# WKV recurrence in chunks: 126 steps with a head against 128 steps with carries in a spare row

## The chip, the cores and the metric

The kernel runs on one core of a Trainium2 chip. The metric is the device time in microseconds (us), the median over runs; a profile of one execution gives the span of the program's instructions on top of it.

## What is computed

The reference is a recurrence over time, for each of 16 batches and 256 columns, with a running maximum that keeps the exponentials in range:

```python
batch, seq_len, d_model = (16, 2048, 256)
for b in range(batch):
    aa = 0; bb = 0; pp = -1e38              # state: numerator, denominator, exponent
    for t in range(seq_len):
        kk = k[b, t]; vv = v[b, t]
        ww = u + kk
        qq = maximum(pp, ww)
        e1 = exp(pp - qq); e2 = exp(ww - qq)
        output[b, t] = (e1 * aa + e2 * vv) / (e1 * bb + e2 + 1e-08)
        ww = pp - w + kk                    # the reference's own recurrence
        qq = maximum(ww, kk)
        e1 = exp(ww - qq); e2 = exp(kk - qq)
        aa = e1 * aa + e2 * vv
        bb = e1 * bb + e2
        pp = qq
```

Note that kk is added to the exponent of the old state too, so the exponent of a state entry is a running sum of k and w. Inputs and output are fp32, 33.6 MB each for k, v and the output.

## The kernel before

Time lies on the partitions, batch and column on the free axis. A chunk is TC = 126 time steps, two halves of HS = 63; 2048 = 16 x 126 + 32, and the first 32 steps are a "head", worked three batches' groups at a time on 96 partitions. A pair is four batches of one chunk, a tile of 126 rows by 1024 columns (128 rows are loaded, two of them replaced). So there are two pairs for the head and four for each of the 16 chunks: 66 pairs, and the main loop has one slot for each, then ten more for the outputs, which run LAG = 9 slots behind.

In one slot n of the loop, in the order of the source, which is also the order on each engine's own queue:

- load(n + 3): two transfers of 512 KB, k and v, issued by GpSimd (L106).
- exps(n), ScalarE (L238): exp of 2048 columns of X, from PSUM, to bf16. X holds two sets of exponents, one as seen from later steps (E) and one with u for the step itself (Z).
- gather_factors (L295, L301), every second slot: rows 126 and 127 of ez, which hold the factors over a half, go by SyncE's transfers to 64 partitions by 64 columns.
- sums(n - 1), TensorE (L279): four one-hot matmuls add the sums of ez and ez*v over each half into one PSUM tile, a row for each.
- round_k(n + 1), VectorE (L219): k to the rounded fp32 form that TensorE takes.
- num(qp, 0), den(q), recip(q), mult(qp, 0), num(qp, 1), mult(qp, 1): the outputs of older pairs, qp = n - 10 and q = n - 9. den and num are matmuls with a triangular matrix and the identity (L399, L417), recip is Ln and Exp on ScalarE (L407, L408), mult the product on VectorE (L428). num has a single PSUM buffer.
- times_v(n), VectorE (L254): ez * v for both sets.
- store, every second slot: 1008 KB, by GpSimd (L444).
- logs(n + 1), TensorE (L227): the exponents as a matmul of k, w and u with constant matrices; X has one buffer of four PSUM banks.
- cast_v(n + 1), VectorE (L246): v to bf16.

Between these stand the steps of the state, spread over the slots after a chunk's last pair by the table `later`: copy_sums (VectorE, L306, and four transfers L311 from rows to 64 partitions), state_logs, state_weights and inject_logs on ScalarE, state_offsets and inject_min on VectorE (L331 to L335, L370, L372), state_chain and inject on GpSimd (L355 to L360, L383), and at the end eight transfers (L387) that write the carries into rows 126 and 127 of the chunk's own ez tiles, from where den and num take them up. [...]

```python
work = [(s + 1, "sums", copy_sums), (s + 2, "exp", state_logs), (s + 2, "dve", state_offsets),
        (s + 2, "act", state_weights), (s + 3, "pool", state_chain)]
if c >= 0:
    work += [(s + 3, "act", inject_logs), (s + 4, "first", inject_min),
             (s + 4, "exp", inject_weights), (s + 4, "pool", inject)]
```

Of the kernel before, what the change touches and what calls it, by code (L numbers as in the profile page):

```python
# [7 lines left out]
F32 = mybir.dt.float32  # L8
# [4 lines left out]

# [3 lines left out]
def kernel(  # L23
# [13 lines left out]
    HS = 63  # L37
    TC = 2 * HS
    T0 = T % TC
    NST = T // TC  # L40
    D = 2 * Dm
    GB = T0
    NG = 3
    NH = NG * GB
    AHEAD = 3
    LAG = 9
    RS = 2.0 ** -43
    LNRS = 43 * 0.6931471805599453
    CAP = 68.0

    consts = ctx.enter_context(tc.tile_pool(name="consts", bufs=1))
    kpool = ctx.enter_context(tc.tile_pool(name="kpool", bufs=AHEAD + 1))
    vpool = ctx.enter_context(tc.tile_pool(name="vpool", bufs=AHEAD + 1))
    vbpool = ctx.enter_context(tc.tile_pool(name="vbpool", bufs=2))
    ezpool = ctx.enter_context(tc.tile_pool(name="ezpool", bufs=6))
    rpool = ctx.enter_context(tc.tile_pool(name="rpool", bufs=3))
# [6 lines left out]
    pst = ctx.enter_context(tc.tile_pool(name="pst", bufs=1, space=bass.MemoryType.PSUM))  # L63
# [4 lines left out]
    pairs = [("head", 0), ("head", 1)]  # L68
    for c in range(NST):
        for p in range(4):  # L70
            pairs.append((c, p))
    NP = len(pairs)
    kr_of, vr_of = {}, {}

    def is_head(n):
        return n < 2

    def tiles_of(n):
        return 1 if n == 1 else 2

    def head_view(x, g):
        b = 6 * g
        e = min(b + 6, B)
        return e - b, x[b:e, 0:T0, :].rearrange("n t d -> t n d")

    def load(n):
        kr = kpool.tile([128, 4, Dm], F32, tag="kr", name="kr")
        vr = vpool.tile([128, 4, Dm], F32, tag="vr", name="vr")
        kr_of[n], vr_of[n] = kr, vr
        if is_head(n):  # L90
            if n == 1:
                K(DVE.memset(kr[64:96, 0:2, :], 0.0))
                K(DVE.memset(vr[64:96, 0:2, :], 0.0))
            for t, x, eng in ((kr, k, SP), (vr, v, SC)):
                for g in range(NG):
                    b = 6 * g + 4 * n
                    e = min(b + 2 * tiles_of(n), B)
                    if b < e:
                        K(eng.dma_start(out=t[g * GB:(g + 1) * GB, 0:e - b, :],
                                        in_=x[b:e, 0:T0, :].rearrange("n t d -> t n d")))  # L100
        else:
            c, p = pairs[n]
            t0 = T0 + c * TC
            r = min(128, T - t0)
            for t, x in ((kr, k), (vr, v)):
                K(POOL.dma_start(out=t[0:r, :, :],  # L106
                               in_=x[4 * p:4 * p + 4, t0:t0 + r, :].rearrange("n t d -> t n d")))

    crow = opool.tile([128, 8, Dm], F32, tag="ot", name="crow")[:, 0:4, :]
    K(DVE.memset(crow[96:128], 0.0))  # L110
    load(0)
    for r, x in ((NH, w), (NH + 1, u), (TC, w), (TC + 1, u)):
        K(POOL.dma_start(out=crow[r:r + 1, :, :], in_=bass.AP(
            tensor=x.tensor, offset=x.offset, ap=[[0, 1], [0, 4], list(x.ap[0])])))
    for n in range(1, AHEAD):
        load(n)


    M1 = consts.tile([128, 128], F32, tag="M1", name="M1")
    I1 = consts.tile([128, 128], F32, tag="I1", name="I1")  # L120
    cc = consts.tile([128, 8], F32, tag="cc", name="cc")
    GE, NE = ALU.is_ge, ALU.not_equal

    def select(ap, cmp, fill, base, cm, n, step):
        K(POOL.affine_select(out=ap, in_=ap, pattern=[[step, n]], compare_op=cmp,
                             fill=fill, base=base, channel_multiplier=cm))

    IO = consts.tile([128, 128], F32, tag="IO", name="IO")
    IOh = consts.tile([128, 128], F32, tag="IOh", name="IOh")
    K(POOL.memset(M1, -1.0))  # L130
    select(M1, GE, 0.0, -1, -1, 128, 1)
    K(POOL.memset(I1, 0.0))
    select(I1, NE, 1.0, 0, -1, 128, 1)
    K(POOL.memset(cc, 0.0))
    for j, r in enumerate((NH, NH + 1, TC, TC + 1)):
        select(cc[:, j:j + 1], NE, 1.0, r, -1, 1, 0)
    K(POOL.memset(cc[:, 4:5], 0.5))
    select(cc[:, 4:5], GE, 0.0, -HS, 1, 1, 0)
    select(cc[:, 4:5], GE, 0.0, TC - 1, -1, 1, 0)
    K(POOL.iota(IOh[:, 0:NH], pattern=[[0, NG], [1, GB]], base=0, channel_multiplier=0,  # L140
                allow_small_or_imprecise_dtypes=True))
    K(POOL.iota(IO[:, 0:TC], pattern=[[0, 2], [1, HS]], base=0, channel_multiplier=0,
                allow_small_or_imprecise_dtypes=True))
# [7 lines left out]
    def head_blocks(f):  # L151
        fill(f[0:GB, GB:NH], 0.0)
        fill(f[GB:2 * GB, 2 * GB:NH], 0.0)

    def step_matrices(name, rows, N, io):
        E, Z = matrix("NLE" + name, F32R), matrix("NLZ" + name, F32R)
        cw, cu = cc[:, rows:rows + 1], cc[:, rows + 1:rows + 2]
        K(DVE.scalar_tensor_tensor(E[:, 0:N], io[:, 0:N], cw, M1[:, 0:N], ALU.mult, ALU.add))  # L160
        K(DVE.scalar_tensor_tensor(Z[:, 0:N], I1[:, 0:N], cu, E[:, 0:N], ALU.add, ALU.add))
        K(DVE.tensor_scalar(E[:, 0:N], E[:, 0:N], cw, None, ALU.add))
        return E, Z

    NLEh, NLZh = step_matrices("h", 0, NH, IOh)
    for f in (NLEh, NLZh):
        head_blocks(f)
        fill(f[:, NH:128], 0.0)
    for g in range(NG):
        fill(NLEh[g * GB:(g + 1) * GB, NH + g:NH + g + 1], 0.5)  # L170
    K(DVE.tensor_single_scalar(NLEh[96:98, NH:NH + NG], cc[96:98, 0:1].broadcast_to([2, NG]),
                               -0.5 * GB, op=ALU.mult))
    kms = [consts.tile([128, 4, Dm], F32R, tag=f"km{j}", name=f"km{j}") for j in range(2)]
    for t in kms:
        K(DVE.tensor_copy(t[96:128, :, :], crow[96:128, :, :]))

    def more_matrices():
        NLE, NLZ = step_matrices("", 2, TC, IO)
        for f in (NLE, NLZ):
            fill(f[0:HS, HS:TC], 0.0)  # L180
            fill(f[:, TC:128], 0.0)
        K(DVE.tensor_single_scalar(NLE[96:128, TC:128], cc[96:128, 2:3].broadcast_to([32, 2]),
                                   -0.5 * HS, op=ALU.mult))
        fill(NLE[0:HS, TC:TC + 1], 0.5)
        K(DVE.scalar_tensor_tensor(NLE[:, TC + 1:128], cc[:, 2:3], -0.5 * HS, cc[:, 4:5], ALU.mult, ALU.add))
        OHh = consts.tile([128, 256], BF16, tag="OHh", name="OHh")
        fill(OHh, 0.0)
        for g in range(NG):
            fill(OHh[g * GB:(g + 1) * GB, 128 + 3 * g:129 + 3 * g], 1.0)
        OH = consts.tile([128, 256], BF16, tag="OH", name="OH")  # L190
        fill(OH, 0.0)
        fill(OH[0:HS, 128:129], 1.0)
        fill(OH[:, 136:137], 1.0)
        fill(OH[0:HS, 136:137], 0.0)
        Id, IdN, Lh, LhN, Lf, LfN = [matrix(x, BF16) for x in ("Id", "IdN", "Lh", "LhN", "Lf", "LfN")]
        K(DVE.tensor_copy(Id, I1))
        K(DVE.tensor_single_scalar(IdN, I1, RS, op=ALU.mult))
        for t, s in ((Lh, 1.0), (LhN, RS)):
            K(DVE.tensor_single_scalar(t, M1, -s, op=ALU.mult))
            head_blocks(t)  # L200
            fill(t[:, NH:128], 0.0)
        Lx = matrix("Lx", F32)
        K(DVE.tensor_scalar(Lx, M1, -1.0, None, ALU.mult))
        fill(Lx[0:HS, HS:TC], 0.0)
        K(DVE.tensor_scalar(Lx[:, 0:HS], Lx[:, 0:HS], cc[:, 2:3], None, ALU.add))
        K(DVE.tensor_scalar(Lx[:, HS:TC], Lx[:, HS:TC], cc[:, 3:4], None, ALU.add))
        fill(Lx[:, TC:128], 0.0)
        K(DVE.tensor_copy(Lf, Lx))
        K(DVE.tensor_single_scalar(LfN, Lx, RS, op=ALU.mult))
        return NLE, NLZ, OHh, OH, Id, IdN, Lh, LhN, Lf, LfN  # L210


    EZ, X_of, KM = {}, {}, {}

    def round_k(n):
        r = NH if is_head(n) else TC
        i = 2 * tiles_of(n)
        KM[n] = kms[n % 2]
        K(DVE.tensor_copy(KM[n][0:r, 0:i, :], kr_of.pop(n)[0:r, 0:i, :]))  # L219

    def logs(n):
        kr = NH + 2 if is_head(n) else 128
        X = psx.tile([128, 2, 2, D], F32, tag="X", name="X")
        km = KM.pop(n).rearrange("p (i n) d -> p i (n d)", i=2)
        for q, m in enumerate((NLEh, NLZh) if is_head(n) else (NLE, NLZ)):
            for i in range(tiles_of(n)):
                K(PE.matmul(X[:, q, i, :], m[0:kr, :], km[0:kr, i, :], start=True, stop=True))  # L227
        X_of[n] = X
# [303 lines left out]
```

## Time and profile before

| | |
|---|---|
| median of 3 runs | 427.45 us (424.86 to 434.87) |
| span in the profile | 419.5 us |
| mean granted clock of TensorE | 0.898 of full speed |
| moved by DMA | 103.84 MB, mean 248 GB/s |
| first and last start of exps (L238) | 14.9 and 371.1 us |

The share of an engine is its busy time over the span; DMA is given as the mean share of the core's 16 DMA engines. In the rows of 40 slices a digit is a tenth of busy time in a fortieth of the span. A group's line gives its source line, engine, operation, output and input with shapes, count, then busy time in all and the mean of one in ns, and last how long its engine had been idle just before and what ended that. A line of the waits reads: who waited, for whom, us in total, how often, the longest.

### The profile page before, as it was taken

The numbers are of one execution on the slowest core, as the hardware profiler recorded it, in microseconds if no ns is written. First come the engines' busy times: TensorE is split into PE (matmuls) and PEld (weight loads), VectorE is DVE, ScalarE is ACT, GpSimd is POOL, SyncE is SP. The second block draws the span as 40 slices with busy tenths as digits, with TensorE's granted clock in tenths as the row PEclk, the third lists the DMA queues.
The fourth block names the chain that finished last, engine by engine and source line by source line (L and its number), as shares of the span: only waits on it lengthen the run. The fifth ranks groups of instructions, "written<-read, shape, count | busy, mean of one in ns | idle before, by whom it ended". The sixth has DMA issues, their size and how long they took to land.

```text
span 419.5 us, 4065 instructions
## 1 busy us (share of the span) xinstructions
PE 281.7 (67%) x1048; PEld 130.5 (31%) x1048; DVE 291.7 (70%) x513; ACT 270.0 (64%) x265; POOL 218.1 (52%) x282
## 2 busy tenths in 40 slices
PE   0367677669695682959587685878686646776660
PEld 0233233334252331424233332433333313332220
DVE  3977698778785783878586784978787726753531
ACT  1245579678784774777575785777788716664760
POOL 7235568575653825475563827475747607041210
PEclk9998799998989897999989696989899986886996
DMA  8498596999989694989889696989898975813444
GB/s 205 157 321 271 161 298 171 297 302 289 325 260 337 188 326 147 300 288 306 284 257 333 202 326 214 310 295 306 291 306 296 268 247 163 240 32 119 163 147 152
DMA packets 43871, 103.84 MB, mean 248 GB/s; under 512 B 18248, under 2 KB 19288, under 8 KB 43848
## 3 DMA queue, kind: packets, MB, share of 16 engines
q0 software_dynamic: 28592, 100.65, 73.9%
q1 hardware_dynamic: 14664, 2.42, 3.7%
q10 hardware_dynamic: 592, 0.52, 0.6%
q8 instruction: 8, 0.13, 0.1%
q14 instruction: 15, 0.12, 0.1%
HBM read 68.11 MB, written 33.55 MB: 242 GB/s over the span
## 4 chain that ended last, share of the span: by engine, by line
DMA 41%; DVE 13%; POOL 12%; PE 11%; SPq 8%; issue 7%; ACT 6%; POOLq 0%; DVEq 0%; ACTq 0%
DMA ez<-ab 19%; DMA tsum<-ts 19%; SPq L387 5%; PE X L227 4%; ACT ez L238 4%; DVE ot L428 3%; DMA fac<-ez 3%; POOL da L359 3%; PE tot L279 3%; POOL ab L383 3%; POOL tb L355 3%; PE num L417 2%; SPq L311 2%; DVE ez L254 2%; POOL AB L360 2%
## 5 line engine op out<-in xcount | busy, mean ns | idle before, releaser
L238 ACT ACTIVATE ez<-X 128x2048 bf16<-128x2048 f32 x66 | 122.0, 1849 | 33.2 <-PE X L227 33.1
L417 PE MATMUL num<-ez,LfN 128*128 128x512 bf16 x128 | 52.2, 408 | 86.5 <-DVE ot L428 73.9
L428 DVE TENSOR_TENSOR ot<-num,rd 126x512 f32<-126x512 f32 (+1 forms) x131 | 89.3, 682 | 25.2 <-PE num L417 19.3
L254 DVE TENSOR_TENSOR ez<-ez,vb 126x2048 bf16<-126x2048 bf16 (+1 forms) x66 | 80.2, 1216 | 22.4 <-ACT ez L238 22.4
L407 ACT ACTIVATE rd<-den 126x1024 f32<-126x1024 f32 (+1 forms) x66 | 66.6, 1009 | 33.5 <-PE den L399 33.3
L444 POOL DMA_DIRECT2D out_dram<-ot x32 | 37.0, 1156 | 95.8 <-DVE ot L428 80.6
L279 PE MATMUL tot<-ez,OH 126*128 126x512 bf16 x256 | 75.2, 420 | 1.1 <-DVE ez L254 1.1
L408 ACT ACTIVATE rd<-rd 126x1024 f32<-126x1024 f32 (+1 forms) x66 | 69.4, 1051 | 2.1
L227 PE MATMUL X<-km,NLE 128*128 128x512 f32 x128 | 58.5, 541 | 15.1 <-ACT ez L238 15.1
L106 POOL DMA_DIRECT2D kr<-in_k_dram x64 | 59.4, 929 | 3.1 <-DVE NLE L160 2.7
L106 POOL DMA_DIRECT2D vr<-in_v_dram x64 | 51.2, 800 | 12.3 <-DVE vb L246 12.3
L417 PE MATMUL num<-ez,IdN 126*128 126x512 bf16 (+1 forms) x131 | 53.4, 408 | 0.0
L219 DVE CAST km<-kr 126x1024 fp32r<-126x1024 f32 (+1 forms) x66 | 45.4, 688 | 3.5 <-DMA kr<-in_k_dram 3.5
L246 DVE CAST vb<-vr 126x1024 bf16<-126x1024 f32 (+1 forms) x66 | 47.4, 718 | 0.4 <-DMA vr<-in_v_dram 0.4
L355 POOL TENSOR_TENSOR tb<-tsum,g 64x256 f32<-64x256 f32 x16 | 12.2, 762 | 66.1 <-DMA tsum<-ts 60.9
L399 PE MATMUL den<-ez,Lf 128*128 128x512 bf16 x128 | 39.9, 394 | 8.9 <-DMA ez<-ab 8.9
L227 PE MATMUL X<-km,NLZ 128*128 128x512 f32 x128 | 45.8, 444 | 0.0
L417 PEld LDWEIGHTS <-IdN 126*128 126x128 bf16 (+1 forms) x131 | 13.3, 101 | 102.1 <-issue 96.5
L399 PE MATMUL den<-ez,Id 126*128 126x512 bf16 (+1 forms) x131 | 41.4, 398 | 0.0
L227 PEld LDWEIGHTS X<-km,NLE 128*128 128x128 f32 x128 | 26.6, 220 | 33.9 <-ACT ez L238 25.0
L365 ACT ACTIVATE y<-AB 64x128 f32<-64x128 f32 x16 | 4.9, 308 | 46.9 <-POOL AB L360 46.9
L279 PEld LDWEIGHTS <-OH 126*128 126x128 bf16 x256 | 21.8, 107 | 40.2 <-issue 27.6
(78 smaller groups left out, 210.3 us busy)
## 6 DMA issues: line engine op xcount, KB each, us to landing
out_dram<-ot POOLq DMA_DIRECT2D x32, 1008.0 KB, 7.6
kr<-in_k_dram POOLq DMA_DIRECT2D x60, 512.0 KB, 8.0
vr<-in_v_dram POOLq DMA_DIRECT2D x60, 512.0 KB, 8.2
ez<-ab SPq DMA_DIRECT2D x128, 4.0 KB, 7.9
kr<-in_k_dram POOLq DMA_DIRECT2D x4, 504.0 KB, 12.1
vr<-in_v_dram POOLq DMA_DIRECT2D x4, 504.0 KB, 13.0
tsum<-ts SPq DMA_DIRECT2D x66, 16.0 KB
fac<-ez SPq DMA_DIRECT2D x64, 4.0 KB, 6.0
```

The lines of the kernel that those rows point to most:

```text
L106: K(POOL.dma_start(out=t[0:r, :, :], in_=x[4 * p:4 * p + 4, t0:t0 + r, :].rearrange("n t d -> t n d")))
L219: K(DVE.tensor_copy(KM[n][0:r, 0:i, :], kr_of.pop(n)[0:r, 0:i, :]))
L227: K(PE.matmul(X[:, q, i, :], m[0:kr, :], km[0:kr, i, :], start=True, stop=True))
L238: K(SC.activation(ez_of(n)[:, 0:2], X_of.pop(n)[:, :, 0:i, :], ACT.Exp))
L246: K(DVE.tensor_copy(vb[0:r, 0:i, :], vr_of.pop(n)[0:r, 0:i, :]))
L254: K(DVE.tensor_mul(ez[0:r, 2:4], ez[0:r, 0:2], vb[0:r, 0:i, :].unsqueeze(1).broadcast_to([r, 2, i, D])))
L279: K(PE.matmul(TOT[c], oh[0:r, 128 - row:256 - row], ez_of(n)[0:r, 2 * q, i, :], start=n == first_of(c) and i == 0 and q == 0, stop=n == la ...
L399: K(PE.matmul(d[:, i, :], m[0:r, :], ez_of(n)[0:r, q, i, :], start=q == 0, stop=q == 1, skip_group_check=True))
L407: K(SC.activation(rd[0:r, 0:i, :], DEN.pop(n)[0:r, 0:i, :], ACT.Ln, scale=RS))
L408: K(SC.activation(rd[0:r, 0:i, :], rd[0:r, 0:i, :], ACT.Exp, scale=-1.0))
L417: K(PE.matmul(d, m[0:r, :], ez_of(n)[0:r, q, i, :], start=q == 2, stop=q == 3, skip_group_check=True))
L428: K(DVE.tensor_mul(o[0:r, 2 * (n % 2) + i, :], NUM.pop((n, i))[0:r, :], RD[n][0:r, i, :]))
```

## The change

The head goes: 2048 = 16 x 128, with halves of 64 steps, and all tiles have 128 rows. The exponents are taken about the middle of each half, so that w and u are no longer rows of the k tile; they come into X by four small matmuls with one or two rows each, in four row strips of the array (CO, WU). The carry of a half is written into the half's own last row (63 and 127), which no later step of the half reads from ez. All ez tiles are in a ring of 12 pairs.

The state is put on 128 partitions (state columns) by TensorE: sums are made once a chunk in four column strips, copied, turned by four fp32 matmuls with a selection matrix (turn), worked on ScalarE and VectorE, turned back by four bf16 matmuls (turn_back), and written into the rows by four transfers. GpSimd does no arithmetic in the loop. Loads are issued six slots ahead; of the v loads, the odd pairs from the ninth on are cast to bf16 by the transfer itself. Stores are one for each pair. The loop's order is changed: logs(n + 1) and round_k(n + 2) come before the second product.

```diff
-    HS = 63
+    HS = 64
     TC = 2 * HS
-    AHEAD = 3
+    NP = 4 * NST
+    RING = 12
+    AHEAD = 6
     LAG = 9
-    kpool = ctx.enter_context(tc.tile_pool(name="kpool", bufs=AHEAD + 1))
-    vpool = ctx.enter_context(tc.tile_pool(name="vpool", bufs=AHEAD + 1))
-    vbpool = ctx.enter_context(tc.tile_pool(name="vbpool", bufs=2))
-    ezpool = ctx.enter_context(tc.tile_pool(name="ezpool", bufs=6))
-    rpool = ctx.enter_context(tc.tile_pool(name="rpool", bufs=3))
+    kpool = ctx.enter_context(tc.tile_pool(name="kpool", bufs=AHEAD))
+    vpool = ctx.enter_context(tc.tile_pool(name="vpool", bufs=6))
+    vbpool = ctx.enter_context(tc.tile_pool(name="vbpool", bufs=4))
+    rpool = ctx.enter_context(tc.tile_pool(name="rpool", bufs=2))
...
+    def v_mode(n):
+        return "dve" if n < 8 or n % 2 == 0 else "dma"
...
+        if v_mode(n) == "dma":
+            vb = vbpool.tile([128, 4, Dm], BF16, tag="vb", name="vb")
+            K(POOL.dma_start(out=vb, in_=src[1]))
...
+    load(0, SP, SC)
+    for r, x in ((0, w), (1, u)):
+        for g in range(4):
+            K((SP if r == 0 else SC).dma_start(out=wuf[32 * g + r:32 * g + r + 1, :, :], in_=bass.AP(
+                tensor=x.tensor, offset=x.offset, ap=[[0, 1], [0, 2], list(x.ap[0])])))
+    load(1, SP, SC)
...
+        for q in range(2):
+            for i in range(2):
+                g = 32 * (2 * q + i)
+                K(PE.matmul(X[:, q, i, :], CO[g:g + 1 + q, :], WU[g:g + 1 + q, :], start=True, stop=False,
+                            tile_position=(g, 0), skip_group_check=True))
+        for q, m in enumerate((NLE, NLZ)):
+            for i in range(2):
+                K(PE.matmul(X[:, q, i, :], m, km[:, i, :], start=False, stop=True, skip_group_check=True))
...
+    def sums(c):
+        t = psm.tile([128, D], F32, tag="misc", name="tot")
+        for p in range(4):
+            for j in range(4):
+                q, i = divmod(j, 2)
+                K(PE.matmul(t[32 * j:32 * j + 32, :], mats["OH"][:, 8 - 2 * p:40 - 2 * p],
+                            ez(4 * c + p)[:, 2 * q, i, :], start=p == 0, stop=p == 3,
+                            tile_position=(0, 32 * j), skip_group_check=True))
...
+    def turn(c):
+        TS = psm.tile([128, 6, 4, 8], F32, tag="misc", name="TS")
+        ts = st.pop((c, "ts"))
+        for b in range(4):
+            K(PE.matmul(TS[:, :, b, :], ts[:, 128 * b:128 * b + 128], mats["Sel"], start=True, stop=True,
+                        skip_group_check=True))
...
+    def state_offsets(c):
+        ...
+        for h in range(2):
+            K(DVE.tensor_add(A[:, 6 + h, :], last[:, 5, :] if h == 0 else A[:, 4, :], nF[:, h, :]))
+            K(DVE.scalar_tensor_tensor(A[:, 4 + h, :], LL[:, 0, 2 * c + 2 + h, :], -1.0, A[:, 6 + h, :],
+                                       ALU.mult, ALU.min))
+        K(DVE.tensor_sub(A[:, 0:2, :], A[:, 4:6, :], A[:, 6:8, :]))
+        K(DVE.tensor_scalar(A[:, 2:4, :], A[:, 6:8, :], -1.0, CAP, ALU.mult, ALU.min))
...
+    def turn_back(c):
+        CT = psm.tile([128, 128], F32, tag="misc", name="CT")
+        for b in range(4):
+            K(PE.matmul(CT, CB_of[c % 2][:, b, :], mats["Id"], start=b == 0, stop=b == 3, skip_group_check=True))
+    def inject(c):
+        cb = small.tile([128, 128], BF16, tag="cb", name="cb")
+        K(DVE.tensor_copy(cb, st.pop((c, "CT"))))
+        r0 = 4 * c % RING
+        for q in range(2):
             for h in range(2):
+                r, x = HS * h + HS - 1, 32 * (2 * q + h)
+                K(SP.dma_start(
+                    out=EZR[r:r + 1, 2 * (1 - q), r0:r0 + 4, :, :].rearrange("o p i (b x) -> o (p i b) x", b=4),
+                    in_=cb[x:x + 32, :]))
...
+        for slot, where, f in ((s + 1, "pe", sums), (s + 1, "dve", copy_sums),
+                               (s + 2, "pe0", turn), (s + 2, "act", state_logs), (s + 2, "dve", state_offsets),
+                               (s + 3, "act", state_weights), (s + 3, "dve", state_chain),
+                               (s + 4, "pe0", turn_back), (s + 4, "dve0", inject)):
...
         if live:
             exps(n)
+        small_work(n, "pe0")
+        small_work(n, "act")
+        small_work(n, "dve0")
         if out_qp:
             num(qp, 0)
         if out_q:
             den(q)
             recip(q)
         if out_qp:
             mult(qp, 0)
             num(qp, 1)
+        if n + 1 < NP:
+            logs(n + 1)
+        if n + 2 < NP:
+            round_k(n + 2)
         if out_qp:
             mult(qp, 1)
             store(qp)
+        if live:
+            times_v(n)
         if n + 1 < NP:
-            logs(n + 1)
             cast_v(n + 1)
+        small_work(n, "pe")
+        small_work(n, "dve")
```

## The prediction

> **What bounds the kernel now.** I read the page first, then the waits, then one long stretch from the middle, then the groups and transfers. No engine is full over the span:
>
> ```profile
> PE 281.7 (67%) x1048; PEld 130.5 (31%) x1048; DVE 291.7 (70%) x513; ACT 270.0 (64%) x265; POOL 218.1 (52%) x282
> DMA  8498596999989694989889696989898975813444
> q0 software_dynamic: 28592, 100.65, 73.9%
> q1 hardware_dynamic: 14664, 2.42, 3.7%
> ```
>
> The DMA row is the nearest to a bound: many slices at 9 in the middle, 1 to 5 at the end. The large transfers take 0.739 x 419.5 = 310 us for 100.65 MB, which is 325 GB/s when busy. 126 steps of all batches ("a chunk", four slots of the loop) are 6.26 MB, 19.3 us; the small transfers of the second queue add 0.037 x 419.5 / 16 = 1.0 us. So DMA needs 20.3 us for a chunk. What a chunk really takes is read from the middle, eleven chunks from one inject_logs to another:
>
> ```profile
> 92.10:341.20 249.10, 182.15 (x704) 86.66 (x704) 187.54 (x308) 179.25 (x176) 142.41 (x173) 0.91 0.88 281
> ```
>
> That is 22.65 us for a chunk, with VectorE busy 17.05, ScalarE 16.3 and DMA 19.9 (0.88). The remaining idle time is in the waits over the whole span:
>
> ```profile
> POOL tb L355 <- DMA tsum<-ts: 60.9, 13, 11.7
> ACT y L365 <- POOL AB L360: 46.9, 15, 9.2
> DVE m L370 <- ACT y L365: 42.8, 15, 8.8
> DVE ez L254 <- ACT ez L238: 22.4, 34, 1.7
> DVE ot L428 <- PE num L417: 19.3, 18, 3.5
> DVE ts L306 <- PE tot L279: 13.8, 13, 1.5
> PE den L399 <- DMA ez<-ab: 8.9, 7, 2.8
> ```
>
> The first three lines are one chain: the sums travel by DMA to another layout, GpSimd waits for them, ScalarE for GpSimd, VectorE for ScalarE. Since all queues are in order, everything behind stands still, 2.9 us a chunk on VectorE, and behind the waiting GpSimd stand the loads. Prices that I use:
>
> ```profile
> L428 DVE TENSOR_TENSOR ot<-num,rd 126x512 f32<-126x512 f32 (+1 forms) x131 | 89.3, 682 | 25.2 <-PE num L417 19.3
> L254 DVE TENSOR_TENSOR ez<-ez,vb 126x2048 bf16<-126x2048 bf16 (+1 forms) x66 | 80.2, 1216 | 22.4 <-ACT ez L238 22.4
> L246 DVE CAST vb<-vr 126x1024 bf16<-126x1024 f32 (+1 forms) x66 | 47.4, 718 | 0.4 <-DMA vr<-in_v_dram 0.4
> L306 DVE COPY ts<-tot 32x512 f32<-32x512 f32 x17 | 11.5, 677 | 13.8 <-PE tot L279 13.8
> L227 PEld LDWEIGHTS X<-km,NLE 128*128 128x128 f32 x128 | 26.6, 220 | 33.9 <-ACT ez L238 25.0
> ez<-ab SPq DMA_DIRECT2D x128, 4.0 KB, 7.9
> ```
>
> [...]
>
> **The change part by part.**
>
> *Head and size.* 64 slots with inputs and 128 rows in place of 66 with 126. [...] the two head slots go, the first exp at 14.9 us and the third at 23.4. The w and u terms become four matmuls of one or two rows before the four X matmuls. The X block takes 1.0 us of TensorE in the middle (181.2 to 182.25); [...] I take 0.8. X has one buffer, so in the first slots, where no output work lies beside it, exp (1.86) then X (1.8) then a semaphore or two make 4.0 us a slot instead of 3.2 to 3.6.
>
> *Sums.* Four one-hot matmuls a slot (0.22 us apart, 3.5 us a chunk) become sixteen in four column strips once a chunk[...]. TensorE gets freer; it is not the bound.
>
> *State.* Off go the 12 tsum and fac transfers a chunk, the fac rows, and the GpSimd arithmetic; so the three waits at the head of the list vanish, and GpSimd only issues transfers, six slots ahead. On VectorE the old state (0.68+0.25+0.54+0.18+2x0.22+0.26+0.29) is 2.63 us a chunk. The new one: the copy of the sums 0.68[...]
>
> *Casts.* 28 of the 64 v loads are cast by the transfer, two a chunk: VectorE loses 2 x 0.65 (operations follow each other some 0.06 sooner than their durations). [...]
>
> *New waits.* turn (four fp32 matmuls) stands first in its slot on TensorE and waits for copy_sums, the last of VectorE's slot before; behind it stand num, den and X, and VectorE's first product waits for num. Each turn has at least one fp32 weight load (0.2), [...] I take 1.4, and 0.6 for num: 2.0 us of VectorE idle a chunk. turn_back (four small bf16 matmuls, about 0.4 and a semaphore) is exposed in the same way: 0.6. The carries go by four transfers in place of eight; their issues follow each other 0.86 us apart (eight took 6.80 in the tail), so the last lands 2.6 + 7.9 = 10.5 us after the first. den of that chunk comes two slots after inject, 10.4 us less 0.9 spent on turn_back and the copy: a wait of about 1 us on TensorE, of which VectorE feels 0.6. Waits for ScalarE and num of the present kind: 0.6 of the present (22.4+19.3+13.8)/16 = 3.5, because products, casts and ez are interleaved so that num has a cast beside it. Sum 17.0 + 2.0 + 0.6 + 0.6 + 0.6 = 20.8 us a chunk.
>
> *DMA.* 12 x 0.524 MB a chunk are 6.29 MB, 19.4 us, and 0.3 for the carries if a casting transfer costs what its 512 KB read costs: 19.7, just below the 20.8. From half the write to twice the time, the two casts are -1.6 to +3.2 us.
>
> *Start.* kr, vr, w and u are now issued by SyncE and ScalarE first; WU needs all eight small rows, issued by some 5.5 us and landed about 5 later (crow took 4.9); then WU copy, km and X: first exp at 14 us, as before. Slot 9 starts at 14 + 9 x 4.0 = 50 us. The other kernel's slot 11 (same data) had its exp at 55.7.
>
> *Tail.* Before, the last exp starts at 371.1 and the end is at 419.5: 48.4 us for ten slots of outputs, with a state chain and a carry transfer inside. The slots stay (2.9 us each where unhindered); turn and turn_back replace the sums' transfers; the wait for the last carries stays, since den follows two short slots later; the last store is half as big, 2 us less. 46.5.
>
> Sum: 50 + 54 slots x 5.2 + 46.5 = 377 us of span. The median time lies 8 us above the span now (427.45 and 419.5): 385.
>
> **The rivals.** (a) *DMA becomes the only bound* because the new waits hide beside each other: 19.7 a chunk, 1.1 x 13.5 chunks less, 370 us. For it: the present kernel runs 21.3 us chunks at 0.94 DMA share around 300 us; against: the turn waits come on an in-order TensorE. (b) *Casting transfers are slow*, twice a plain one: 22.9 us of DMA a chunk, +2.1 x 13.5, 413 us. Nothing in the profile speaks on it. (c) *The new waits are larger*: turn 4 us, carries 2 us, chunk 23.5: +36, 421 us, no change. For it: VectorE's small chain is all dependent operations, each with a semaphore. (d) *Slower*: the carries land as late as the slowest now (12.1 us) in every chunk with TensorE in order behind them, and fp32 turns run at half clock (PEclk has slices at 6): chunk 25, +57, 442 us. Against: den and num wait for carries only 13.8 us in all now, with twice as many transfers.
>
> **How the numbers follow.** Forecast 0.55, (a) 0.17, (b) 0.12, (c) 0.09, (d) 0.07. Faster by over 2% are the forecast, (a) and (b): 0.84; within 2%: 0.09; slower: 0.07. The range from 367 to 414 takes in (a), the forecast with a chunk of 19.7 to 22.5, and (b).
>
> **What would show it.** Right: no wait on a sums transfer, GpSimd without arithmetic, DVE around 17 us a chunk of 20 to 21.5, an idle stretch of VectorE ahead of the product in the slot of turn near 2 us, first exps 4 us apart, DMA above 0.9 in the middle. The steps would be wrong if vb loads take much longer than kr loads to land, if VectorE waits for km or vb, if the wait on carries exceeds 2 us a chunk, or if VectorE's small state operations exceed 5 us a chunk.

## The result, and the profile after

The changed kernel takes 403.77 us (median of 4, 401.16 to 405.58) beside 426.15 us for the kernel before (4 runs): ratio 0.948, 95% interval 0.9422 to 0.9537. The forecast was 385 us. The profiled execution has a span of 399.2 us. First the busy times, the granted clock, the DMA row and the transfer queues:

```profile
PE 286.8 (72%) x1449; PEld 133.9 (34%) x1472; DVE 283.7 (71%) x559; ACT 260.6 (65%) x225; POOL 158.9 (40%) x203
...
PEclk9999857996999889999969999988999996999896
DMA  7978975699899989999989899997999991333344
...
q0 software_dynamic: 37824, 91.24, 78.2%
q1 hardware_dynamic: 4144, 1.59, 1.7%
```

GpSimd lost its arithmetic in the loop (218.1 to 158.9 us, now the issuing of transfers and some set-up), and the second queue moves 1.59 MB instead of 2.42. VectorE's total hardly moved, as forecast. The 91.24 MB count a casting transfer at the 256 KB that it writes.

By stretch (columns: the window, its length, then busy time of PE, PEld, DVE, ACT and POOL, the granted clock, the DMA share and GB/s); the start, a chunk, the next chunk, and eleven chunks from one Ln of the state to another:

```profile
15.60:62.60 47.00, 27.69 (x104) 14.38 (x108) 27.27 (x55) 17.41 (x11) 16.14 (x25) 0.84 0.81 237
172.20:193.20 21.00, 16.19 (x91) 7.71 (x92) 17.22 (x33) 16.21 (x15) 10.17 (x12) 1.00 0.97 275
193.20:216.00 22.80, 18.57 (x91) 8.37 (x92) 17.22 (x33) 16.16 (x15) 10.18 (x12) 0.85 0.90 255
84.65:322.78 238.13, 187.57 (x996) 87.99 (x1012) 189.50 (x363) 178.19 (x155) 111.98 (x132) 0.94 0.94 269
```

One caution on the clock: the profile's first record of it lies at about 44 us, and the figure counts what lies before as 1.00 (from 15.60 to 44.00 us it reads 1.00), so the four 9s at the head of PEclk and the 0.84 are too high. How the first slots really ran is read from the matmuls, under "The start" below.

The mean chunk is 238.13 / 11 = 21.65 us, against 22.65 before. It is made of two kinds: seven chunks of 21.0 us at full clock and four of 22.8, in which the granted clock falls to 0.50 for about 7 us. VectorE does 17.22 us in both. Its timeline through one 21.0 us chunk (start, duration, operation, and in brackets the idle time before it and who ended that) shows where most of the other 3.8 us are:

```profile
170.30 0.69 DVE L225 COPY ts<-tot 128x512 f32<-128x512 f32 x1 [0.73 <-PE tot L218]
172.66 0.69 DVE L316 TENSOR_TENSOR ot<-num,rd 128x512 f32<-128x512 f32 x1 [1.67 <-PE num L309]
...
183.04 0.29 DVE L280 CAST cb<-CT 128x128 bf16<-128x128 f32 x1 [0.49 <-PE CT L275]
183.53 0.69 DVE L316 TENSOR_TENSOR ot<-num,rd 128x512 f32<-128x512 f32 x1 [0.20 <-PE num L309]
```

1.67 us ahead of the first product in the slot of turn, 0.69 around the turn back, and 0.73 for the sums; the rest, 0.6 us, is in gaps of 0.03 to 0.08 us between operations. The waits over the whole span have the same places (who waited, for whom, us, times, longest); no line names a transfer of sums or carries any more:

```profile
DVE ot L316 <- PE num L309: 44.5, 46, 1.8
PE num L309 <- DVE ot L316: 34.6, 33, 1.8
...
PE CT L275 <- DVE CB L268: 25.8, 16, 2.2
...
ACT LL L237 <- PE TS L232: 17.5, 16, 1.8
...
PE TS L232 <- DVE ts L225: 12.9, 16, 0.9
```

By parts, from exp to exp: the start up to slot 9's exp 62.6 us, 54 slots in 291.5 us, the tail 45.1. In the kernel before, the same data are in slot 11. The prediction gives 55.7 us for its exp, but that is slot 10's; slot 11's is the next:

```profile
55.67 1.85 ACT L238 ACTIVATE ez<-X 128x2048 bf16<-128x2048 f32 x1
...
58.81 1.88 ACT L238 ACTIVATE ez<-X 128x2048 bf16<-128x2048 f32 x1
```

So before, the start took 58.8 us, the same 54 slots 312.3 and the tail 48.4: the middle gives 21 us and the tail 3, and the start takes 4 back.

### The profile page after: what moved, and what is told of

Read it like the earlier page. It is cut to its first block, busy times and chain, and to the rows that moved or that the text cites. A ratio compares the mean times of both kernels' runs of the same rounds, so it can differ in the third digit from the quotient of the medians.

```text
span 399.2 us, 4440 instructions
## 1 busy us (share of the span) xinstructions
PE 286.8 (72%) x1449; PEld 133.9 (34%) x1472; DVE 283.7 (71%) x559; ACT 260.6 (65%) x225; POOL 158.9 (40%) x203
## 3 DMA queue, kind: packets, MB, share of 16 engines
q0 software_dynamic: 37824, 91.24, 78.2%
q1 hardware_dynamic: 4144, 1.59, 1.7%
q10 hardware_dynamic: 1072, 1.06, 0.9%
## 4 chain that ended last, share of the span: by engine, by line
PE 34%; DVE 29%; issue 21%; DMA 7%; ACT 4%; POOL 3%; POOLq 0%; DVEq 0%
DVE EZR L196 10%; PE num L309 10%; PE X L174 7%; DVE ot L316 7%; PE den L296 6%; DMA kr<-in_k_dram 4%; PE tot L218 3%; ACT EZR L178 3%; PE TS L232 3%; POOL out_dram L321 3%; DVE vb L191 3%; PE X L170 3%; DVE ts L225 2%; DMA out_dram<-ot 1%; DMA vr<-in_v_dram 1%
## 5 line engine op out<-in xcount | busy, mean ns | idle before, releaser
L178 ACT ACTIVATE EZR<-X 128x2048 bf16<-128x2048 f32 x64 | 120.0, 1875 | 51.7 <-PE X L174 51.4
L316 DVE TENSOR_TENSOR ot<-num,rd 128x512 f32<-128x512 f32 x128 | 88.3, 690 | 53.7 <-PE num L309 44.5
L302 ACT ACTIVATE rd<-den 128x1024 f32<-128x1024 f32 x64 | 65.2, 1019 | 51.3 <-PE den L296 51.3
L196 DVE TENSOR_TENSOR EZR<-EZR,vb 128x2048 bf16<-128x2048 bf16 x64 | 77.8, 1216 | 5.4 <-ACT EZR L178 5.3
L309 PE MATMUL num<-EZR,LN 128*128 128x512 bf16 x121 | 49.0, 405 | 35.2 <-DVE ot L316 34.6
L303 ACT ACTIVATE rd<-rd 128x1024 f32<-128x1024 f32 x64 | 67.9, 1061 | 2.0
L66 POOL DMA_DIRECT2D kr<-in_k_dram x62 | 55.7, 899 | 16.9 <-DVE km L161 14.8
L161 DVE CAST km<-kr 128x1024 fp32r<-128x1024 f32 x64 | 44.0, 688 | 8.6 <-DMA kr<-in_k_dram 6.1
L309 PE MATMUL num<-EZR,IdN 128*128 128x512 bf16 x114 | 46.3, 406 | 0.4
L296 PE MATMUL den<-EZR,Id 128*128 128x512 bf16 x128 | 40.9, 403 | 0.1
L296 PE MATMUL den<-EZR,L 128*128 128x512 bf16 x126 | 40.4, 403 | 0.7
## 6 DMA issues: line engine op xcount, KB each, us to landing
kr<-in_k_dram SPq DMA_DIRECT2D x2, 512.0 KB, 14.3
```

The source lines that it names most:

```text
L66: K((kq or POOL).dma_start(out=kr, in_=src[0]))
L161: K(DVE.tensor_copy(km, kr_of.pop(n)))
L178: K(SC.activation(ez(n)[:, 0:2], X_of.pop(n), ACT.Exp))
L196: K(DVE.tensor_mul(ez(n)[:, 2:4], ez(n)[:, 0:2], vb.unsqueeze(1).broadcast_to([128, 2, 2, D])))
L296: K(PE.matmul(d[:, i, :], mats[m], ez(n)[:, q, i, :], start=q == 0, stop=q == 1, skip_group_check=True))
L302: K(SC.activation(rd, DEN.pop(n), ACT.Ln, scale=RS))
```

## The experiments

My theory was that VectorE's in-order loop sets the chunk, with the two turns exposed in it, and that the start's slots and the half-clock chunks are what the forecast missed. Its chief rival was that the transfers, at 0.97 of 16 engines in the 21.0 us chunks, bound the middle already. Times are medians; ratios are to the kernel before, and that of the changed kernel is 0.948. The kernel before ran anew beside each group of experiments, with medians from 420 to 426 us, so a difference between two experiments can come out some 6 us apart by the medians and by the ratios.

### Are the transfers a floor?

```diff
     later = {}
-    for c in range(NST):
+    for c in range(0):
```

> Leaves out the whole state: no sums, no turns, no logs and offsets, no carries, so each chunk is computed as if nothing came before it. Transfers of k, v and outputs are unchanged. VectorE then has 17.2 less about 4.0 us of work a chunk, 13.2. Theory (the transfers are a floor just under the changed kernel's chunk, 20.4 us busy of 21.0): the chunk falls from a mean of 21.65 to about 20.3 us and no further, about 18 us less over the middle and some 4 us less in the tail: 22 us in all, ratio about 0.945, with DMA at 0.98 or more in the middle. Rival (the DMA share is a load and not a floor[...]): the chunk falls to what ACT needs, 16.2 us less the small exps, 15 to 18 us, and the time by 45 us or more.

312.66 us, ratio 0.7376 (0.7309 to 0.7443). Four slots of it (the window's columns as above):

```profile
175.30:191.02 15.72, 13.83 (x65) 6.27 (x64) 13.68 (x19) 15.32 (x12) 11.51 (x13) 1.00 1.10 366
```

The same k, v and output bytes went through in 15.72 us at 366 GB/s, where the changed kernel was 0.97 "busy" with 275 GB/s in 21.0 us. ScalarE is all but full now, 15.32 us of 15.72: its three large operations are 1.87 + 1.02 + 1.06 = 3.95 us a slot. So the rival holds: the DMA share is no floor, it can even exceed 1, and my expectation of 20.3 us was wrong. The state with its waits is worth 91 us.

### What do the turns cost?

Both turns late, first as a pair behind the second num, with the copy of the carries behind the second product:

```diff
-        small_work(n, "pe0")
-        small_work(n, "act")
-        small_work(n, "dve0")
         if out_qp:
             num(qp, 0)
...
             num(qp, 1)
+        small_work(n, "pe0")
+        small_work(n, "act")
         if n + 1 < NP:
             logs(n + 1)
...
             store(qp)
+        small_work(n, "dve0")
```

> The turns of the sums and of the carries move in their slot from ahead of the den and num matmuls to behind the second num (ahead of the next logs), ACT's small work with them, and the copy of the carries on VectorE to behind the second product. In a 21.0 us chunk of the changed kernel VectorE idles 1.67 us ahead of the first product in the turn's slot and 0.69 us around the turn back. Theory (VectorE's loop bounds the middle, and the exposed turns are idle time of it): up to 2.4 us a chunk less, at most down to the 20.4 us in which the transfers were busy, so 0.6 us a chunk at the least bound and 2 at the most: 8 to 25 us less over 13.5 chunks, most likely about 10. Rival A (the transfers at 0.97 busy bound the 21.0 us chunks already): VectorE's idle time only moves to another wait, change under 3 us. Rival B (the turn now delays the logs of the next slot, so ACT's exp waits for X): the time grows by about 1 us a chunk, 13 us.

395.81 us, ratio 0.9326 (0.9223 to 0.9429): 8 us less, near the size of the theory, but with a new line among the waits:

```profile
PE den L296 <- DMA EZR<-cb: 29.0, 14, 3.5
```

The carries now leave later, and den waits for them: part of what was won was given back, and the middle of the profile, 288.2 us, is only 3 us shorter than the changed kernel's. So the turn of the carries was put between den and the second num, its copy behind the first product:

```diff
-                               (s + 2, "pe0", turn), (s + 2, "act", state_logs), (s + 2, "dve", state_offsets),
+                               (s + 2, "pe1", turn), (s + 2, "act", state_logs), (s + 2, "dve", state_offsets),
...
-        small_work(n, "pe0")
-        small_work(n, "act")
-        small_work(n, "dve0")
...
             den(q)
             recip(q)
+        small_work(n, "pe0")
         if out_qp:
             mult(qp, 0)
+        small_work(n, "dve0")
+        if out_qp:
             num(qp, 1)
+        small_work(n, "pe1")
+        small_work(n, "act")
```

> As in the run that moved both turns late, the turn of the sums stands behind the second num, but the turn of the carries stands between den and the second num, and the copy of the carries on VectorE directly behind the first product, ahead of the rounding. With both turns late, chunks in which nothing waited for the carries took 18 to 20 us, but den waited 29.0 us in all (14 times) for the carries' transfer. Theory (that wait gave back what the later turn won): the carries leave about 1 us earlier, so the wait falls from 2.1 to about 1 us a chunk, a chunk takes about 19.5 us, and the time is 10 to 14 us below that run, 382 to 387 us. Rival (the transfers at 0.95 busy hold the chunk at 20.4): den waits less, VectorE and ACT wait elsewhere, and the time stays at 395.

354.75 us, ratio 0.846 (0.8399 to 0.8521), 49 us under the changed kernel by the medians, 43 by the ratios, 44.7 between the spans of the two profiles; far more than I expected. Eleven chunks of the middle, and one of them:

```profile
94.21:298.92 204.71, 177.57 (x1013) 85.67 (x1012) 185.37 (x364) 175.31 (x154) 108.62 (x129) 1.00 1.02 306
225.43:243.58 18.15, 16.12 (x93) 7.83 (x92) 16.83 (x34) 15.93 (x15) 10.16 (x13) 1.00 1.06 316
```

A chunk takes 18.61 us on the mean and 18.15 where den does not wait for the carries, with VectorE busy 16.83, and the clock is 1.00 throughout: with most of TensorE's long waits the half-clock stretches went too. The wait for the carries is down from 29.0 us to little:

```profile
PE den L296 <- DMA EZR<-cb: 4.9, 5, 1.9
```

The middle takes 250.4 us, 38 less than with both turns late. The wait for the carries can account for some 24 of these; the rest is not taken apart, but the clock was lower there too, 0.956 on the mean of the profiled execution beside 0.966 here. Then the turn of the sums alone was moved, in the same way:

```diff
-                               (s + 2, "pe0", turn), (s + 2, "act", state_logs), (s + 2, "dve", state_offsets),
+                               (s + 2, "pe1", turn), (s + 2, "act", state_logs), (s + 2, "dve", state_offsets),
...
         small_work(n, "pe0")
-        small_work(n, "act")
+        if not any(w == "pe1" and m == n for m, w in later):
+            small_work(n, "act")
...
             num(qp, 1)
+        if (n, "pe1") in later:
+            small_work(n, "pe1")
+            small_work(n, "act")
```

> Of the two turns only that of the sums is moved, from ahead of the slot's den and num to behind the second num, with ACT's log behind it; the turn of the carries and its copy stay first in their slot, as in the changed kernel. With both moved, the time was 354.8 us, 49 less than the changed kernel; in the changed kernel VectorE's idle time ahead of the first product is 1.67 us in the slot of the sums' turn and 0.69 us in that of the carries' turn. Theory (each turn costs in proportion to the idle time that it shows, so the sums' turn is some 70% of the 49 us): about 34 us, 370 us in all, between 363 and 377. Rival (the carries' turn, for which TensorE waits 25.8 us in all on CB and holds back num, den and the next logs, is the larger part): 380 to 392.

377.49 us, ratio 0.8949 (0.8889 to 0.9009): 26 of the 49 us by the medians, between the theory and the rival. An undisturbed chunk of it:

```profile
256.23:275.46 19.23, 15.93 (x91) 7.86 (x92) 17.13 (x34) 15.98 (x14) 10.19 (x13) 1.00 1.03 301
```

So in undisturbed chunks the sums' turn cost 21.0 - 19.2 = 1.8 us, about its 1.67 us of idle VectorE, and the carries' turn 19.23 - 18.15 = 1.1, more than its 0.69: VectorE's busy time fell by 0.3 us as well. Of the 44.7 us between the profiles 41.1 lie in the middle, 3.04 a chunk: 2.85 from the two turns, 0.65 from the half-clock stretches, which are gone, less 0.46 for the chunks in which den still waits. The tail gives 2.9. With one turn moved, a stretch from 196 to 217 us in the profile still has a clock of 0.92; with both, the eleven chunks have 1.00. The expectation failed because it shared out the 49 us by idle time alone.

### The half-clock chunks

```diff
         X_of[n] = X
+        if n >= 10:
+            d = psd.tile([128, 2, D], F32, tag="den", name="fill")
+            for j in range(3):
+                K(PE.matmul(d[:, 0, :], NLE, km[:, 0, :], start=True, stop=True, skip_group_check=True))
```

> From pair 10 on, three extra matmuls of the logs' matrix on the rounded k go into the den bank behind each slot's logs (0.66 us of TensorE at full clock); their result is overwritten and used nowhere. In the changed kernel the granted clock falls to 0.50 for about 7 us at a time, five times between 92 and 338 us, and a chunk with such a stretch takes 22.8 us instead of 21.0. Theory (the stretches come from TensorE's idle time and cost what the chunks show): they become rarer or vanish, the mean chunk falls from 21.65 towards 21.0 and the time by 4 to 9 us. Rival (the stretches have another cause, or TensorE's extra 2.6 us a chunk stand in VectorE's way): the stretches stay, and the time grows by up to 9 us.

408.66 us, ratio 0.9721 (0.9601 to 0.9842): 5 us more than the changed kernel by the medians, 10 by the ratios. The stretches vanished from the middle of the profile; two successive chunks:

```profile
188.00:209.98 21.98, 18.95 (x105) 9.98 (x104) 17.39 (x34) 16.38 (x14) 9.69 (x13) 1.00 0.92 266
209.98:231.96 21.98, 18.96 (x105) 10.00 (x104) 17.44 (x34) 16.39 (x15) 9.72 (x13) 1.00 0.94 265
```

So the stretches go with TensorE's idle time, as the theory said: with TensorE busy 18.95 us of a chunk instead of 16.19, all twelve chunks from 86 to 349 us take 22.0 us, and the two shown have a clock of 1.00. But the filling stood in the loop's way, 0.98 us a chunk where the stretches cost 0.65 on the mean, and the time went as the rival said.

### The start

```diff
         X_of[n] = X
+        if n < 10:
+            d = psn.tile([128, D], F32, tag="num", name="fill")
+            for j in range(6):
+                K(PE.matmul(d, NLE, km[:, 0, :], start=True, stop=True, skip_group_check=True))
```

> Six extra matmuls of the logs' matrix on the rounded k, into a bank that nobody reads, follow the logs of each of the first ten slots. Theory (the start's slots take 4.77 us rather than 4.0 because TensorE runs at half clock there, so that each X block takes about 2.8 us instead of 2): with more work on TensorE the granted clock rises and slots 2 to 9 shrink towards 4.0 us in spite of the extra work, slot 9's exp about 4 to 6 us earlier, the whole time 3 to 6 us shorter. Rival A (the packed matmuls that precede the logs cost the time whatever the clock): the extra work, six matmuls of 0.24 us or more, lengthens the slots by up to 1.5 us each, 5 to 12 us longer. Rival B (the ACT and PSUM turn sets the slots, not the matmuls): no change in the slots.

392.77 us, ratio 0.928 (0.92 to 0.9361), more than the 3 to 6 us expected. Nine slots of the start take 39.50 us beside 47.00:

```profile
15.60:55.10 39.50, 32.22 (x155) 21.37 (x154) 27.05 (x55) 17.13 (x12) 16.08 (x23) 1.00 0.92 277
```

That the changed kernel's first slots ran at half clock is seen in its matmuls (start, duration, operation). First an X block at 30 us, where the clock has no record; then a part of one at 60 us, where the record says 0.50; then a block of the middle, at 1.00:

```profile
30.47 0.80 PE L170 MATMUL X<-WU,CO 1*128 1x512 f32 x4 [1.97 <-ACT EZR L178]
31.20 1.22 PE L174 MATMUL X<-km,NLE 128*128 128x512 f32 x2
32.22 1.05 PE L174 MATMUL X<-km,NLZ 128*128 128x512 f32 x2
...
60.51 1.22 PE L174 MATMUL X<-km,NLE 128*128 128x512 f32 x2
...
173.93 0.51 PE L170 MATMUL X<-WU,CO 1*128 1x512 f32 x4
174.37 0.73 PE L174 MATMUL X<-km,NLE 128*128 128x512 f32 x2
174.94 0.63 PE L174 MATMUL X<-km,NLZ 128*128 128x512 f32 x2
```

The block takes 2.80 us in the first slots and 1.64 in the middle. With the extra matmuls it takes 1.63 from 29 us on; the exps then come 3.60 us apart instead of 4.77, and the idle time of ScalarE before each is 1.72 us instead of 2.90. Both rivals fall: neither the packed matmuls nor the turn of the buffers set the 4.77 us, the clock did.

The other edit of the start takes the k block of pair 1 out of SyncE's queue:

```diff
-    load(1, SP, SC)
+    load(1, None, SC)
```

> The k block of pair 1 is issued first in GpSimd's queue instead of by SyncE; nothing else moves. In the changed kernel it was issued at 6.6 us behind the eight small loads of w and u on SyncE, landed 14.3 us later, and the second exp followed the first after 8.2 us where later exps of the start follow after 4.8. Theory (the late k block costs the start what it shows): the second exp comes about 4.8 us after the first, slot 9's exp moves from 62.6 to about 59, and the whole time falls by about 3.4 us, ratio to the changed kernel about 0.992. Rival (the start's loss is made good later, because the transfers bound the middle and they now run no further ahead): the second exp is earlier, the end is not, under 1 us.

Of the eight small loads only the four of w stood ahead of k on SyncE; those of u are issued by ScalarE. The time is 402.55 us, ratio 0.9456 (0.9336 to 0.9577): no difference from the 0.948 that can be told. The start is as the theory has it:

```profile
15.12 1.88 ACT L178 ACTIVATE EZR<-X 128x2048 bf16<-128x2048 f32 x1 [13.03 <-PE X L174]
19.89 1.88 ACT L178 ACTIVATE EZR<-X 128x2048 bf16<-128x2048 f32 x1 [2.90 <-PE X L174]
```

Slot 9's exp came 4.0 us earlier (58.64), but in the profiled execution the middle was 7.5 us longer (299.0 from slot 9's exp to the last), with a lower mean clock, 0.899. All of the 7.5 us lie in its first four chunks; the later ones are as in the changed kernel. It is left open whether that is the edit or the scatter of the clock (0.916 to 0.953 in the changed kernel's runs).

### The casts and the sums' transfer

```diff
-        return "dve" if n < 8 or n % 2 == 0 else "dma"
+        return "dve"
```

> Every v block is loaded as float32 and cast by VectorE; none is cast in its transfer. VectorE gains two casts of 0.69 us in a chunk of four, 1.4 us. Theory (VectorE's loop with the waits that follow it bounds the chunk, the transfers do not): about 1.4 us a chunk longer over 13 chunks, 18 us, ratio to the changed kernel about 1.045. Rival A (the casting transfers cost the 16 DMA engines more than plain ones and the transfers bound): no longer, or shorter. Rival B (the casts fall into VectorE's idle time, 3.8 us a chunk): under 5 us longer.

425.39 us, ratio 1.0141 (1.0087 to 1.0195): 21.6 us more than the changed kernel by the medians, near the theory; both rivals were wrong. Part of it may be the clock, 0.88 on the mean from 111 to 303 us in this run, where eleven chunks of the changed kernel have 0.94. Note that without the casts in the transfer the changed kernel is some 1.4% slower than the one before.

In the kernel before, the sums' transfers were left out:

```diff
+    tsum0 = consts.tile([64, 2, 2, 64], F32, tag="tsum0", name="tsum0")
+    K(DVE.memset(tsum0, 1.0))
...
-        t = small.tile([64, 2, 2, 64], F32, tag="tsum", name="tsum")
...
-                K(SP.dma_start(out=t[:, h, q, :], in_=ts[r:r + 8, :].rearrange("r (x c) -> r x c", c=64)))
-        SUMS[c] = t
+        SUMS[c] = tsum0
```

> The kernel before, with the transfers that bring the sums across partitions left out: the state is computed from a constant tile of ones instead of the sums. All else, the state's 50 us or so of VectorE work and the carries' transfers included, stays. Theory (the waits for the sums' transfer, 60.9 us of VectorE, and what is queued behind them are what the change removes; its own new work costs about 1.3 us of VectorE and 2.4 us of turns a chunk): the chunk falls from about 23.4 us to 18 to 20, the time by 45 to 70 us. Rival (another wait ends right after, so that most of the wait was not on the path, and the change's gain came from the casts and the new chunk layout): the time falls by 20 us or less.

384.88 us, ratio 0.9182 (0.912 to 0.9245): 35 us, between the two expectations. The transfer wait was worth that much, not the 45 to 70 expected. The 60.9 us that the expectation puts down to VectorE are GpSimd's; VectorE's wait at the end of that chain was 42.8. And another wait grew in its place, that for the carries, from 8.9 us:

```profile
PE den L396 <- DMA ez<-ab: 23.0, 9, 6.3
```

And the casts, added to the kernel before (the ring of fp32 v tiles goes from four to three beside it):

```diff
-    vpool = ctx.enter_context(tc.tile_pool(name="vpool", bufs=AHEAD + 1))
+    vpool = ctx.enter_context(tc.tile_pool(name="vpool", bufs=3))
...
+    vcpool = ctx.enter_context(tc.tile_pool(name="vcpool", bufs=3))
...
+        direct = n % 2 == 1 and not is_head(n)
+        kr_of[n] = kr
+        if not direct:
+            vr = vr_of[n] = vpool.tile([128, 4, Dm], F32, tag="vr", name="vr")
+        else:
+            vr = VB[n] = vcpool.tile([128, 4, Dm], BF16, tag="vc", name="vc")
```

> The kernel before with one thing of the change: every second v block outside the head is cast to bf16 in its transfer, into a ring of three tiles, so that VectorE casts 1.4 us less in four slots. The changed kernel without its casting transfers took 425.4 us, 22 us more than with them and 5 more than the kernel before. Theory (the casts are worth the same in both kernels, because VectorE's loop bounds both): 15 to 22 us less than before, about 400 to 405, ratio 0.95 to 0.965. Rival (before, VectorE's freed time only lengthens its wait for the sums' transfer, 60.9 us): less than 6 us, ratio 0.985 or more.

419.47 us (411.69 to 421.72) beside 425.12 (419.44 to 435.46): about 6 us by the medians, in runs too scattered for an interval. The rival is nearer, and the waits show a reason; GpSimd's wait for the sums was 60.9 us:

```profile
POOL tb L360 <- DMA tsum<-ts: 64.4, 14, 10.5
DVE m L375 <- ACT y L370: 51.5, 16, 8.5
```

VectorE's wait behind that chain grew from 42.8 to 51.5 us: 8.7 us of the some 22 that were freed (1.4 a chunk) went there; where the rest went is not shown. So the casts were worth 22 us with the new state layout and about 6 without, and the new layout did not pay without the casts.

### All together

The two edits of the start on top of both turns moved:

> Three edits together: both turns moved as in the run of 354.8 us, the k block of pair 1 issued first by GpSimd, and six extra matmuls behind the logs of the first ten slots. Theory (the start's savings are independent of the middle's): alone, the extra matmuls brought slot 9's exp from 62.6 to 55.1 us and the early k block to 58.6; together about 51.5, so some 10 us less than 354.8: 345 us. Rival (the loads cannot follow a faster start, so the start waits for k or v instead): 350 or more.

348.21 us, ratio 0.8195 (0.8085 to 0.8306), after 0.846 without the two edits. Slot 9's exp is at 51.80, as the sum of the two savings says, and the expected 10 us lie within what the two comparisons give: 6.5 by the medians, 11 by the ratios. In its profile the mean clock from 84 to 250 us was 0.98. With `LAG = 10` in addition:

> As the run with the three edits together, and the outputs one slot further behind the exps: LAG 10 instead of 9, so that den comes a slot later after the carries' transfer. In the run of 354.8 us den waited about 1.33 us a chunk for the carries and VectorE idled 1.4 us behind that. Theory (that wait is on VectorE's path): the middle's chunk falls by up to 1.3 us, 12 to 18 us, and the tail grows by one slot, 3 to 4 us: 10 us less than the run with three edits, about 335. Rival (the ring of 12 is then full up to the last slot, and exp waits for the outputs, or the transfers at over 0.99 bound the middle): no gain, or up to 10 us more.

342.99 us (342.1 to 345.2), ratio 0.8142 (0.8073 to 0.8211), the fastest version, 61 us under the changed kernel by the medians. Four chunks of it:

```profile
155.19:227.84 72.65, 64.03 (x363) 31.27 (x368) 67.35 (x133) 63.76 (x57) 40.70 (x49) 1.00 1.06 321
```

18.16 us a chunk, the same as an undisturbed chunk of the run with both turns moved: later outputs can only remove the chunks in which den did wait for the carries, not shorten the others. The expectation took that wait for 1.33 us in every chunk; that run's list of waits, above, has 4.9 us in five times. The gain over LAG 9 is within the intervals.

## Why the prediction came out as it did

**The direction and the loop were right.** The predicted 20.8 us a chunk, VectorE's 17.0 and 3.8 of waits, is 21.0 in an undisturbed chunk, 17.22 and 3.8. The 17.0 rested on an estimate of mine for the new state's operations, and took it that 128 rows cost VectorE no more than 126: a product of 512 columns takes 690 ns on 128 rows, where before it took 682 on 126 and 676 on 96. The turn's 2.0 was 1.67 of idle VectorE, and 1.8 when taken away; turn_back's 0.6 was 0.69, and 1.1 when taken away. That the waits sum to the same 3.8 is partly luck: the wait for the carries, 0.6, is zero, and 0.6 us of short gaps between the state's and other operations had no term. The four fp32 matmuls of turn took 0.9 us to the next matmul's start, where I took 1.4 as my own estimate; the trace has two records for each. The 0.8 that I took for the w and u matmuls was an estimate too: the four, in four row strips, took 0.44 us, and the two matmuls behind them take 0.57 us to the next start, 0.56 in the kernel before. The sixteen matmuls of sums in four column strips took 1.05 us, as long as four took before (1.04); yet TensorE did not get freer, 286.8 us busy where it was 281.7. The state's operations sum to 4.0 us in the groups; the costliest on 128 columns is the one with scattered bf16 output, 431 ns where a product of 128 columns to fp32 (L261) takes 283:

```profile
L225 DVE COPY ts<-tot 128x512 f32<-128x512 f32 x16 | 11.1, 691 | 16.4 <-PE tot L218 16.4
...
L268 DVE TENSOR_TENSOR CB<-AB,G 128x128 bf16<-128x128 f32 x16 | 6.9, 431 | 0.0
L246 DVE TENSOR_TENSOR A<-A,nF 128x32 f32<-128x32 f32 x32 | 6.1, 192 | 1.1
```

**What was wrong**, in the order of the sum 50 + 54 x 5.2 + 46.5 + 8:

- *Start, 50: 62.6.* The eight slots from the second exp to slot 9's took 38.85 us, 6.9 more than at 4.0. I had taken the X block's 1.0 us from the middle, where the clock is full; in the first slots TensorE waits 1.97 us of each and stays at half clock, so its block takes 2.8. The extra-matmul run showed this. The second exp came 8.2 us after the first, 4.2 more than my 4.0, because k of pair 1 stood behind four small rows on SyncE, was issued at 6.6 us and took 14.3 us to land; the run with k issued first showed 4.77 there. The first exp came 1.6 late. The 55.7 us that I set beside the 50 were slot 10's; 58.8 would have been right.
- *Middle, 5.2 a slot: 5.40.* 0.65 us a chunk are the half-clock chunks, which the list "what would show it" didn't have; I used PEclk only in the slower rival. The rest is that the undisturbed chunks take 21.0 us where I had 20.8. The wait for the carries is zero: the groups of transfers give 4.8 us to landing, not 7.9, and the four issues take 2.4, together 7.2 of the 9.5 us that I counted until den.

```profile
kr<-in_k_dram POOLq DMA_DIRECT2D x62, 512.0 KB, 6.2
vr<-in_v_dram POOLq DMA_DIRECT2D x34, 512.0 KB, 6.6
vb<-in_v_dram POOLq DMA_DIRECT2D x28, 256.0 KB, 7.2
...
EZR<-cb SPq DMA_DIRECT2D x64, 8.0 KB, 4.8
```

- *Tail, 46.5: 45.1. Offset, 8: 4.6* (403.77 less 399.2). Both small. The offset was misread: a run lies 2 us above its own span (401.16 and 399.2 us; 421.51 and 419.5 before), and the rest of the 8 is that the profiled run was quicker than the median.

These are +12.6, +10.7, -1.4 and -3.4, together the 18.5 us that were missing. That 403.77 still lies in the range is partly luck: the start's 12.6 us had no allowance, and fit because the chunk used little of the one made for it (up to 22.5 us).

**The DMA step was wrong in kind.** I divided bytes by busy time and called 19.7 us a chunk what DMA needs; rival (a) and the worry about slow casting transfers rest on it. The run without the state moved the same blocks in 15.7 us, and the run with both turns moved ran under 19.7 too. For the same k, v and output bytes the DMA engines were busy 0.97 x 21.0 = 20.4 us a chunk in the changed kernel and 1.10 x 15.72 = 17.3 without the state, so busy time is not what the bytes need. Rival (b) falls with it: the casting transfers land in 7.2 us, near a plain block's 6.6, VectorE never waits for them, and taking them away costs 22 us by the medians.

**What the forecast did not see** is how much the waits could be avoided. It counted the turns as the price of the layout. They were the price of standing first in an in-order queue: with the sums' turn behind the second num and the carries' turn behind den, VectorE idles 1.3 us in an undisturbed chunk instead of 3.8.

## What to carry to other kernels

A small step that waits for the previous slot's last result should not stand at the head of its slot on an in-order engine; put it behind the work that feeds the bounding engine (403.77 us became 354.75 here), and check that the late end doesn't arrive too late for its own consumer (with both turns behind the second num, den waited 29.0 us for the carries). Don't take the DMA busy share for a floor (0.97 at 275 GB/s here, and 1.10 at 366): look at GB/s in a stretch where transfers run freely, or leave other work out and see how fast the same bytes go. Where TensorE idles much of every slot, as in the start here (1.97 us of 4.77, with an X block of 2.80 us beside 1.64 in the middle), price its work at half clock too, and check the clock by the durations of like matmuls: the profile's figure says nothing of the time before its first record, at 44 us here.

## What the runs showed of the hardware

The 16 DMA engines carried 366 GB/s at a share of 1.10, and were at 0.97 with 275: the share hardly tells the load.

In the changed kernel the clock's falls to 0.50 begin at about 92, 137, 201, 266 and 331 us and last 6.8 us; the last three gaps are 65 us, three chunks, though each chunk has the same idle times. The longest idle stretch of TensorE ahead of these falls is 1.75 to 1.78 us, and ends 1 to 2 us before each. With both turns moved, and TensorE's longest wait in an ordinary chunk at 0.94 us, the eleven chunks of the middle stayed at 1.00; with the start's edits added, the 0.98 from 84 to 250 us means some 6.6 us at half clock, about one such fall. A wait of that length alone doesn't bring a fall: in the changed kernel's chunk from 172.20 to 193.20 us, all at 1.00, TensorE waited 1.77 us up to 178.64 and 1.79 up to 182.61, and with both turns late it waited 2.07 us up to 241.29, while the X blocks behind, at 243.50 and 247.91 us, took 1.63 and 1.62 us, as at full clock. What brings a fall is left open.
